# Down's first products by a second level of 2x2 blocks, shorter norm roots, and a shared last addition

## The chip, the cores and the metric

The kernel runs on one core of a Trainium2 chip. A core has five engines that run side by side: TensorE (PE in the profile, with its weight loads as PEld) for matmuls, VectorE (DVE) and ScalarE (ACT) for elementwise work, GpSimd (POOL), and SyncE (SP), which here only issues transfers. SP, ACT and POOL each have a queue of DMAs, served in order. Matmuls write to PSUM, everything else lives in SBUF or in DRAM. The metric is the device time of one execution in microseconds (us); lower is better. The three runs of the kernel before took 2181.01 to 2182.33 us, with a median of 2181.39.

## The reference

One residual block over 2048 tokens with 1024 channels, in float32:

```python
h = rmsnorm(x, norm_mix_pre)
u_pool, u_glu, g_a, g_b = split(h @ w_in)
branch_a = pool_mixer(u_pool, ...)        # windowed means, small maps, projection
branch_b = conformer_conv(u_glu, ...)     # GLU, causal convolution, layernorm, silu, projection
merged = sigmoid(g_a) * branch_a + sigmoid(g_b) * branch_b
x = x + rmsnorm(merged @ w_o, norm_mix_post)
h = rmsnorm(x, norm_mlp_pre)
f = square(relu(h @ w_up)) @ w_down       # 1024 -> 4096 -> 1024
x = x + rmsnorm(f, norm_mlp_post)
```
`rmsnorm(x, g)` is x divided by the root of (mean of squares + EPS), times g, with EPS = 1e-6.

## The kernel before

Data lie with channels on the 128 partitions and tokens along the row; a tile is 128x1024 float32, 512 KB. The tokens are two blocks b of 1024, each of two halves t of 512. A float32 product is made of three fast passes: each operand is split into a high part (a cast to fp32r on ACT, `wh` or a first `big`/`tr`) and a low part (the difference, a `sub` on DVE, `wl` or the second), and high x high, high x low, low x high are added in PSUM. `product` issues such a product of a 2x2 block of weights with a 1024-row slice of tokens: 24 matmuls of 128x512 (line 268).

Large matrix products are also made by a seven-product scheme over 2x2 blocks: seven products of sums and differences of blocks instead of eight products of blocks. `ORDER` gives the order of the seven. The products of w_in, of the output projection (wo) and of up are grouped so in `Octet`s, with block sums of the weights in `ws` tiles; up makes 8 octets for each b, and its relu-squared results go to DRAM as `fd[b, u, (m, t)]`, some of them already as the sums `t1`, `t2`, `t3`, `t4` that down wants.

Down runs for both blocks together. Its seven products i of the outer scheme are each summed over four slabs s of 1024 hidden rows, for two output halves o and two blocks b: 7 x 4 x 2 x 2 = 112 products. `SHARED` = (1, 5, 6, 3, 7) run for both b with one set of weights, `ALONE` = (4, 2) after them; the list `jobs` holds the order. `token_cells` loads and splits the token operands of a job two jobs ahead, `weight_down` the weights, `down_product` multiplies, and `last_product` joins the seven results into the four quarters c00, c01, c11, u. One job, `FILL`, is done early by `filler` to give PE work between wo and up of b=1; its result waits in DRAM. Half of the accumulators are pairs of `rb` tiles from the small PSUM pool, which is why products of down stand as `PE rb L268` in places.

The order of the work: the program is written in the main line of PE's products, and `ordered` and `mark` pin that line. Everything beside it (convolution, norms, `scales` for the mlp norm) is in `Lane`s of generators that `bg` moves on by some steps after every product. A scheduler orders each engine's instructions by priority; `tc.high_priority(offset=AHEAD)` moves a load or split ahead. Each engine and each queue then runs strictly in its order. `load` issues on SP's queue, `store` on ACT's, `aside` on POOL's. SBUF tiles come from pools with fixed numbers of buffers (`pbig` 28, `ptr` 9, `pfo` 5, `pwr` 4 for weights as loaded, `pwh` and `pwl` 3 for their parts).

Norm roots: `Squares` adds up squares, `root_acc` sums over partitions by 128x1 matmuls, `root_dve` makes 1/root by 8 to 14 small DVE operations (a bit trick and two refinements), `spread_dve` and `spread_pe` spread it over the partitions by matmuls with the identity, in a high and a low part. Finally `at_end` does the last product in two halves of 256 tokens with warming matmuls (`idle`) between, and then the last post norm and residual: for each of four output tiles a multiplication by the root (`times`) and an addition of x (`plus`), all on DVE, and a store on SP's queue.

## Time and profile before

| what | value |
|---|---|
| median of 3 runs | 2181.39 us (2181.01 to 2182.33) |
| the profiled execution's own time | 2180.6 us |
| its span in the trace | 2178.8 us |
| PE busy | 2159.4 us, 99% |
| DVE, ACT, POOL busy | 1614.7, 1017.8, 16.4 us |
| transferred | 552.33 MB, mean 253 GB/s |
| up of b=1 in the trace | 1243.27 to 1556.79 us |
| products i=1 of down | 1556.79 to 1632.95 us |

In rows of the profile, an operation reads `out<-in` by the program's names, with line, engine and shape; in square brackets stands the time that the engine was idle before it and what ended that. A row of a stretch gives its length, then busy time and instructions of PE, PEld, DVE, ACT and POOL, then the granted TensorE clock (1.00 is full), the busy share of the DMA engines and GB/s. The profiled execution took 2180.6 us, 1.8 more than the span of its instructions.

### The profile page before, as it was taken

Reading aid. Unit: us, or ns where it says so; the run is one execution under the profiler, and the core shown is the slowest. Engines: PE = TensorE matmul, PEld = TensorE weight load, DVE = VectorE, ACT = ScalarE, POOL = GpSimd, SP = SyncE. Lnnn points to the kernel's source line nnn. Section 1 sums busy time; section 2 is a strip of 40 time slices with the busy share of each in tenths; the row PEclk is TensorE's granted clock in tenths of the full one; section 3 lists DMA queues with packets and bytes.
Section 4 is the critical chain, followed back from the end, with each engine's and each line's share of the span. In section 5 each row is a group of like instructions: output and inputs, shape, how many; then the busy total and the mean of one; then the engine's idle time right before and its main releaser. Section 6 shows DMA issues by size and latency. Waiting matters only on the chain.

```text
span 2178.8 us, 25059 instructions
## 1 busy us (share of the span) xinstructions
PE 2159.4 (99%) x9678; PEld 1788.4 (82%) x9678; DVE 1614.7 (74%) x1593; ACT 1017.8 (47%) x1064; POOL 16.4 (1%) x39
## 2 busy tenths in 40 slices
PE   9999999999999999999999999999999999999998
PEld 7888888888888888888888878888888888888887
DVE  8997789998688998977757765756744746546786
ACT  6444454334543445555635775555622323334551
POOL 1000000000000000000000000000000000000000
PEclk9999999999999999999999999999999999999999
DMA  7688997778997788445787685644977875545882
GB/s 274 233 297 311 325 353 272 269 252 292 340 379 239 262 306 287 158 148 198 279 300 268 214 286 189 228 168 160 322 275 274 320 271 178 209 154 188 275 301 86
DMA packets 155625, 552.33 MB, mean 253 GB/s; under 512 B 17264, under 2 KB 19568, under 8 KB 155504
## 3 DMA queue, kind: packets, MB, share of 16 engines
q1 hardware_dynamic: 139696, 493.99, 63.7%
q10 hardware_dynamic: 12672, 46.14, 5.5%
q0 software_dynamic: 3136, 10.58, 1.3%
q8 instruction: 76, 1.25, 0.2%
q14 instruction: 45, 0.37, 0.1%
HBM read 366.00 MB, written 184.64 MB: 253 GB/s over the span
## 4 chain that ended last, share of the span: by engine, by line
PE 93%; DVE 3%; DMA 2%; issue 1%; ACT 1%; SPq 0%; DVEq 0%
PE up L268 26%; PE down L268 23%; PE wo L268 8%; PE ga L268 7%; PE gb L268 7%; PE glu L268 6%; PE rb L268 5%; PE B L268 4%; PE A L268 4%; PE pool L268 3%; DMA big<-xt 1%; PE rb L563 1%; DVE big L121 1%; PE mix L268 1%; DVE y L938 0%
## 5 line engine op out<-in xcount | busy, mean ns | idle before, releaser
L268 PE MATMUL up<-big,wh 128*128 128x512 f32 x1792 | 481.0, 390 | 2.2 <-DVE big L121 1.6
L268 PEld LDWEIGHTS up<-big,wh 128*128 128x128 f32 x1792 | 335.8, 188 | 74.0 <-DVE big L121 2.7
L225 ACT CAST wh<-wr 128x1024 fp32r<-128x1024 f32 x195 | 204.9, 1052 | 384.9 <-PE up L268 77.4
L938 DVE SCALAR_TENSOR_TENSOR y<-v,cst,y 128x1024 f32<-128x1024 f32 x240 | 307.2, 1280 | 2.8
L268 PE MATMUL up<-big,wl 128*128 128x512 f32 x896 | 276.1, 389 | 0.0
L268 PE MATMUL down<-big,wh 128*128 128x512 f32 x736 | 274.9, 389 | 0.0
L225 ACT CAST wh<-ws 128x1024 fp32r<-128x1024 f32 x126 | 132.4, 1052 | 252.8 <-PE up L268 63.6
L268 PE MATMUL down<-tr,wh 128*128 128x512 f32 x616 | 239.7, 389 | 0.0
L121 DVE TENSOR_TENSOR tr<-tr,big 128x1024 fp32r<-128x1024 f32 x100 | 120.5, 1222 | 117.3 <-ACT big L1730 116.8
L268 PE MATMUL down<-big,wl 128*128 128x512 f32 x664 | 204.5, 389 | 0.0
L121 DVE TENSOR_TENSOR wl<-ws,wh 128x1024 fp32r<-128x1024 f32 x118 | 143.9, 1220 | 75.5 <-ACT wh L225 75.3
L268 PEld LDWEIGHTS up<-big,wl 128*128 128x128 f32 x896 | 168.1, 188 | 34.8
L121 DVE TENSOR_TENSOR wl<-wr,wh 128x1024 fp32r<-128x1024 f32 x118 | 143.7, 1218 | 53.7 <-ACT wh L225 52.9
L1730 ACT CAST big<-tr 128x1024 fp32r<-128x1024 f32 x98 | 101.2, 1050 | 169.5 <-DMA tr<-fd 138.1
L268 PEld LDWEIGHTS down<-big,wh 128*128 128x128 f32 x736 | 138.2, 188 | 28.6
L268 PEld LDWEIGHTS down<-big,wl 128*128 128x128 f32 x664 | 124.6, 188 | 25.9
L268 PEld LDWEIGHTS down<-tr,wh 128*128 128x128 f32 x616 | 115.6, 188 | 24.0
L268 PE MATMUL wo<-big,wh 128*128 128x512 f32 x480 | 128.7, 390 | 0.0
L268 PE MATMUL glu<-big,wh 128*128 128x512 f32 x464 | 126.8, 394 | 1.2 <-DVE big L816 0.5
L268 PE MATMUL gb<-big,wh 128*128 128x512 f32 x448 | 120.0, 390 | 0.0
L268 PE MATMUL ga<-big,wh 128*128 128x512 f32 x448 | 120.0, 389 | 0.0
L268 PEld LDWEIGHTS wo<-big,wh 128*128 128x128 f32 x480 | 89.9, 188 | 18.5
(212 smaller groups left out, 3351.4 us busy)
## 6 DMA issues: line engine op xcount, KB each, us to landing
tr<-fd SPq DMA_DIRECT2D x110, 512.0 KB, 5.1
wr<-w_down SPq DMA_DIRECT2D x90, 512.0 KB, 5.8
wl<-kept SPq DMA_DIRECT2D x85, 512.0 KB, 4.6
kept<-wl SPq DMA_DIRECT2D x72, 512.0 KB, 6.1
wr<-w_up SPq DMA_DIRECT2D x64, 512.0 KB, 4.4
wr<-w_in SPq DMA_DIRECT2D x60, 512.0 KB, 5.3
fd<-tr ACTq DMA_DIRECT2D x54, 512.0 KB, 3.9
fd<-tr SPq DMA_DIRECT2D x46, 512.0 KB, 2.9
```

The lines of the kernel that those rows point to most:

```text
L121: return nc.vector.tensor_tensor(o, a, b, op=ALU.subtract)
L225: nc.scalar.copy(hi[:, :n], src[:, :n])
L268: i = nc.tensor.matmul(ps, w[wp][:, (at + k) * P : (at + k + 1) * P], rhs[k][xp], start=start and n == 0, stop=stop and n == len(order) - ...
L563: nc.tensor.matmul(st[:, at + g : at + g + 1], ss[:, g * P : (g + 1) * P], inv_n, start=start is None or (start and g == 0), stop=stop, sk ...
L938: nc.vector.scalar_tensor_tensor(acc, v[:, k : k + TB], wk, acc, op0=ALU.mult, op1=ALU.add)
L1730: nc.scalar.copy(hi, t)
```

## The change

Three parts. **Down.** The 16 products of i=1 (a matrix product of 4x2 slab parts by two token blocks) become a second level of the seven-product scheme: seven products `level_product`, each over two halves n, 14 in all, accumulated in three PSUM tiles x, y, z. Their weight sums are made by `level_weights`, a new generator ahead of `scales` in the lane beside up of b=1, and stored on POOL's queue; their token sums by `fetch_other` and `sink` during the octets of up of b=1 (T1 in octets 0 to 3; T2, T3, T4 in 4 to 7). `SHARED` loses 1, and the early job `FILL` is now (0, 7, 0), whose weights are differences; its result is added to `u` before the job (1, 3, 0). The `t4` sums are stored on POOL's queue instead of SP's, `pfo` has 6 buffers. **Roots.** EPS is added with the squares (or by `root_floor`, small matmuls into the same PSUM tile), `root_dve` takes its input from PSUM and has 8 operations, and one float32 matmul replaces the two fp32r ones in spreading. **The end.** Of the last half's four additions two go to GpSimd, one is split in two with a store for each half on ACT's and SP's queue, and two products by the root go to PSUM; four warming matmuls fewer.

```diff
-IDLE = (7, 9)
+IDLE = (7, 5)
...
+        h = step(ALU.mult, h, -0.5 * 0.375**3 * scale, a, "s2")
+        return step(ALU.add, h, 1.5 * 0.375 * scale, y, "sy")
+
+    def root_floor(st, b, t, at=0, n=G):
+
+        nc.tensor.matmul(
+            st[:, :n], f32(ident), q2[b, t][:, at : at + n], start=True, stop=False,
+            skip_group_check=True,
+        )
...
             for g in range(dg[0].shape[1]):
-                for i in (0, 1):
-                    j = nc.tensor.matmul(
-                        rb[:, g * P : (g + 1) * P], dg[i][:, g : g + 1].to_broadcast([P, P]), ident,
-                        start=g == 0 and i == 0, stop=i == 1, skip_group_check=True,
-                    )
...
+                j = nc.tensor.matmul(
+                    rb[:, g * P : (g + 1) * P], dg[0][:, g : g + 1].to_broadcast([P, P]),
+                    f32(ident), start=g == 0, stop=True, skip_group_check=True,
+                )
...
+            def fetch_other():
+                h = u - SLABS
+                for k, at in (
+                    (("T3", (1, h, (0, 0))), ("T2", (1, h, "T1")), ("T4", (0, u, (0, 0))))
+                    if u >= SLABS else (("T1", (0, u, (0, 0))),)
+                ):
+                    other[k] = fo()
+                    load(other[k], fd[at])
...
+                if b and (m, t) == (0, 0):
+                    for k, d in other.items():
+                        if k == "T4":
+                            sub(d, d, other["T2"])
+                        else:
+                            sub(d, o, d)
+                        keep(k, d, aside)
...
-    SHARED, ALONE = (1, 5, 6, 3, 7), (4, 2)
+    SHARED, ALONE = (5, 6, 3, 7), (4, 2)
...
-            for n in f.order:
+            for n in f.order[:2]:
                 times(1, n)
-                plus(1, n)
+                x = at(f.x[n], 1)
+                nc.gpsimd.tensor_tensor(x, x, at(f.ready[n], 1), op=ALU.add)
+                load(two(out[f.b, n, f.t])[:, :, HT:], x)
+            scaled = {}
+            for k, n in enumerate(f.order[2:]):
+                scaled[n] = ps[:, k * T : (k + 1) * T].rearrange("p (c t) -> p c t", c=2)
+                mul(
+                    scaled[n], at(f.ready[n], 1),
+                    rbs[1][:, :HT].unsqueeze(1).to_broadcast([P, 2, HT]),
+                )
...
+            for i, queue in enumerate((store, load)):
+                x = at(f.x[c], 1)[:, i]
+                add(x, x, scaled[c][:, i])
+                queue(two(out[f.b, c, f.t])[:, i, HT:], x)
...
-    FILL = jobs.pop(0)
...
+    FILL = (0, SHARED[-1], 0)
+    jobs.remove(FILL)
...
+    def level_product(p, w, cells):
+
+        a = {1: "x", 2: "z", 6: "x", 7: "x", 4: "x", 5: "y", 3: "y"}[p]
+        if p in (1, 2, 5):
+            sums_of[a] = psum("down")
+        ps = sums_of[a]
+        for n in (0, 1):
+            product(
+                ps, w[n], cells[2 * n : 2 * n + 2],
+                start=p in (1, 2, 5) and n == 0, stop=p in (2, 4, 3) and n == 1,
+            )
+            if n == 0:
+                bg()
...
-    then(lambda: lanes.extend([Lane(1, scales())]), octs[1])
+    then(lambda: lanes.extend([Lane(1, chain_of(level_weights(), scales()))]), octs[1], 1)
...
+    w = [level_weight(LEVEL[0], k) for k in (0, 1)]
+    here, coming = coming[0], coming[1:]
+    for n, p in enumerate(LEVEL):
+        with behind():
+            if n + 1 < len(LEVEL):
+                following = [level_weight(LEVEL[n + 1], k) for k in (0, 1)]
+                there = level_parts(coming.pop(0))
...
+            if n + 2 < len(LEVEL):
+                coming.append(level_loads(LEVEL[n + 2], (BIG, TR, BIG, TR, BIG)[n]))
...
+        level_product(p, w, here)
+        w, here = following, there
```

The change moves instructions on the engines. On DVE at the start of up of b=1, where PE waits for the operand differences (rows of L121 that write `big`), the order before has (L121 is a subtraction, L118 an addition, L124 a multiplication; a `tr` row makes a difference of token blocks, the `big` row behind it that operand's low part):

```order
L118 TENSOR_TENSOR big_9476<-big_9476,big_9463 128x1024
L121 TENSOR_TENSOR tr_9811<-big_9509,big_9003 128x1024
L121 TENSOR_TENSOR tr_9822<-big_9565,big_9085 128x1024
L121 TENSOR_TENSOR big_9814<-tr_9811,big_9813 128x1024
L121 TENSOR_TENSOR big_9825<-tr_9822,big_9824 128x1024
L118 TENSOR_TENSOR tr_9855<-tr_9798,tr_9853 128x1024
L121 TENSOR_TENSOR tr_9872<-big_9419,tr_9811 128x1024
L121 TENSOR_TENSOR tr_9883<-big_9463,tr_9822 128x1024
L121 TENSOR_TENSOR big_9875<-tr_9872,big_9874 128x1024
```
and in the changed kernel, at the same place:

```order
L118 TENSOR_TENSOR big_9422<-big_9422,big_9409 128x1024
L121 TENSOR_TENSOR fo_9674<-tr_9707,fo_9674 128x1024
L121 TENSOR_TENSOR tr_9762<-big_9455,big_8959 128x1024
L121 TENSOR_TENSOR tr_9773<-big_9511,big_9041 128x1024
L121 TENSOR_TENSOR big_9765<-tr_9762,big_9764 128x1024
L121 TENSOR_TENSOR big_9776<-tr_9773,big_9775 128x1024
L118 TENSOR_TENSOR tr_9806<-tr_9747,tr_9804 128x1024
L121 TENSOR_TENSOR tr_9826<-big_9369,tr_9762 128x1024
L121 TENSOR_TENSOR tr_9837<-big_9409,tr_9773 128x1024
L121 TENSOR_TENSOR fo_9749<-tr_9806,fo_9749 128x1024
L121 TENSOR_TENSOR big_9829<-tr_9826,big_9828 128x1024
```
The two `fo` rows, the T1 sums of octets 0 and 1, stand between the operands that PE waits for.

On DVE in the first stage of down, the order of one level and the start of the next in the changed kernel (`tr` and `big` rows are the low parts of a level's four token operands, `wl` those of its two weights):

```order
L121 TENSOR_TENSOR tr_12108<-tr_12108,big_12178 128x1024
L121 TENSOR_TENSOR tr_12109<-tr_12109,big_12181 128x1024
L121 TENSOR_TENSOR tr_12110<-tr_12110,big_12184 128x1024
L121 TENSOR_TENSOR wl_12169<-wr_12166,wh_12168 128x1024
L121 TENSOR_TENSOR tr_12111<-tr_12111,big_12187 128x1024
L121 TENSOR_TENSOR wl_12175<-wr_12172,wh_12174 128x1024
L121 TENSOR_TENSOR big_12190<-big_12190,big_12260 128x1024
L121 TENSOR_TENSOR big_12191<-big_12191,big_12263 128x1024
```
Six splits come for each two products there; before, a job of two products had two token splits, and two weight splits for each two jobs.

On DVE at the end, before, from the end of the last root (`sy`, `sp`, `sq`) to the second of four tiles:

```order
L124 TENSOR_TENSOR sy_16352<-sy_16350,q_11137 128x2
L634 CAST sp_16354<-sy_16352 128x2
L121 TENSOR_TENSOR sq_16355<-sy_16352,sp_16354 128x2
L124 TENSOR_TENSOR big_13626<-big_13626,rb_16358 128x2x256
L118 TENSOR_TENSOR big_15547<-big_15547,big_13626 128x2x256
L124 TENSOR_TENSOR big_13654<-big_13654,rb_16358 128x2x256
L118 TENSOR_TENSOR big_15549<-big_15549,big_13654 128x2x256
```
and in the changed kernel (the two additions that are missing, to `big_15599` and `big_15601`, are the last rows on POOL):

```order
L601 SCALAR_TENSOR_TENSOR s_3286_16371<-s_3285_16369,rb_16334 128x2
L601 SCALAR_TENSOR_TENSOR sy_16373<-s_3286_16371,sy_16367 128x2
L124 TENSOR_TENSOR big_13744<-big_13744,rb_16375 128x2x256
L124 TENSOR_TENSOR big_13772<-big_13772,rb_16375 128x2x256
L124 TENSOR_TENSOR down_16094<-big_12246,rb_16375 128x512
L124 TENSOR_TENSOR down_16094<-big_12329,rb_16375 128x512
L118 TENSOR_TENSOR big_15603<-big_15603,down_16094 128x2x256
L118 TENSOR_TENSOR big_15605<-big_15605,down_16094 128x256 x2
```
The four multiplications now stand together, and two additions follow them on DVE.

More of the change, by code (lines that the diff above doesn't have):

```diff
@@ L1762, in to @@
                 mark(add(c[:, h], of[:, h], p))
[L1764 to L1771 removed]
+        if i == 5:
             taken(c11)
@@ new lines, in level_weight, with level_loads @@
+    def level_weight(p, n):
+        with tc.high_priority(offset=AHEAD):
+            t = mk(p_wr, "wr")
+            o = {1: 2 * n, 2: 2 * (n + 2), 4: 2 * (n + 2) + 1}.get(p)
+            load(t, level[p, n] if o is None else w_down[o, 0])
+            return split_w(t)
+    def level_loads(p, home):
+        b, at, k = {
+            1: (0, 0, (0, 0)), 2: (0, SLABS, (0, 0)), 3: (1, SLABS, (0, 0)),
+            5: (1, 0, "T1"), 6: (1, SLABS, "T2"), 7: (1, SLABS, "T3"), 4: (1, SLABS, "T4"),
+        }[p]
+        with tc.high_priority(offset=AHEAD):
+            los = [mk(*home, F32R) for _ in range(SLABS)]
+            for u, lo in enumerate(los):
+                load(f32(lo), fd[b, u + at, k])
+        return los
```

184 lines of the change are left out of this document (116 added, 68 removed).

## The prediction

> **What bounds the kernel now.** I read the page's busy shares and its chain first, then the chain over the place of the change, then PE's waits, and last the engines' load stage by stage.
>
> ```profile
> span 2178.8 us, 25059 instructions
> PE 2159.4 (99%) x9678; PEld 1788.4 (82%) x9678; DVE 1614.7 (74%) x1593; ACT 1017.8 (47%) x1064; POOL 16.4 (1%) x39
> PE 93%; DVE 3%; DMA 2%; issue 1%; ACT 1%; SPq 0%; DVEq 0%
> ```
> PE is busy for all but 19 us of the span and carries 93% of the chain that ended last: the kernel is a queue of matmuls, and a matmul taken out of it is worth its own length as long as its neighbours' operands are there in time. The chain through the first stage of down (columns: start, length, what) prices it:
>
> ```profile
> 1556.79 5.44 PE down L268 x24
> 1562.23 5.44 PE rb L268 x24
> 1567.67 16.32 PE down L268 x72
> ...
> 1627.51 5.44 PE rb L268 x24
> ```
> A product is 24 matmuls in 5.44 us, 0.2267 us each, with no gap to the next one. Products i=1 run here from 1556.79 to 1632.95: fourteen of them in 76.16 us (the other two are the filler's). PE's waits (total, times, longest) show where it does starve:
>
> ```profile
> PE rb L563 <- DVE tr L118: 1.9, 1, 1.9
> PE rb L654 <- DVE sp L634: 1.6, 2, 1.0
> PE up L268 <- DVE big L121: 1.6, 2, 0.8
> ```
> All of it is small. The load by stretch (sum; PE, PEld, DVE, ACT, POOL busy; granted clock, DMA share, GB/s) tells what room is left; the rows are the start of up of b=1, the rest of that up, stage i=1 of down, the rest of down but for its end, and the 22 us in which the DMA moved most:
>
> ```profile
> 1243.27:1297.67 54.40, 52.63 (x236) 42.51 (x235) 43.76 (x48) 42.76 (x49) 0.00 (x0) 1.00 0.83 290
> 1297.67:1556.79 259.12, 259.12 (x1160) 214.86 (x1159) 161.18 (x156) 148.37 (x148) 0.00 (x0) 1.00 0.58 208
> 1556.79:1632.95 76.16, 76.16 (x337) 63.06 (x337) 37.17 (x32) 19.96 (x22) 0.00 (x0) 1.00 0.79 288
> 1632.95:1981.11 348.16, 348.16 (x1537) 288.29 (x1537) 188.98 (x161) 114.66 (x117) 0.00 (x0) 1.00 0.65 227
> 620.76:642.52 21.76, 21.76 (x97) 18.02 (x96) 19.30 (x17) 7.04 (x7) 0.00 (x0) 1.00 1.02 403
> ```
> In the stages that the change loads, DVE was 49% (37.17 of 76.16) and 62% (161.18 of 259.12) busy. Only the start of up is near its limit, 43.76 of 54.40 us, and there PE did wait.
>
> **Products of down.** Sixteen products i=1 become fourteen: two fewer are 48 matmuls, 48 x 0.2267 = **-10.9 us**, and no product has to be added for it. The filler keeps a product for each o, now i=7.
>
> What must hide is the feeding of the seven new levels. In 76 us the queues now move 28 token tiles, 14 weight tiles and about five for the next stage, 47 of 512 KB, 24.6 MB or 324 GB/s; the stage moved 288 and the fullest row above 403, so I cost the transfers at nothing. DVE's work there, by the prices
>
> ```profile
> L121 DVE TENSOR_TENSOR wl<-wr,wh 128x1024 fp32r<-128x1024 f32 x118 | 143.7, 1218 | 53.7 <-ACT wh L225 52.9 <-DMA kept<-wl 0.6
> L225 ACT CAST wh<-wr 128x1024 fp32r<-128x1024 f32 x195 | 204.9, 1052 | 384.9 <-PE up L268 77.4
> ```
> is 42 splits, 3 additions and about 6 operations for the next stage, 51 x 1.22 = 62 us (82%); ACT has 42 casts, 4 copies and 6 more, 52 x 1.05 = 55 us (72%). Both fit, but each level needs four token and two weight splits within two products (10.88 us; DVE 7.3 us), the loads come one or two levels ahead, and every queue works in order: a load that is late delays the splits behind it, and those delay PE. The stretch above with DVE at 80% cost PE 1.77 us (54.40 - 52.63); so between 0 and 2 us for levels and seams, I take **+1.0**.
>
> The sums made in up of b=1 are 16 token subtractions, 16 loads and 16 stores; the weight sums are 8 operations, 8 loads and 8 stores (the stores on POOL's queue, 0.54 us to issue by the row
>
> ```profile
> L131 POOL DMA_DIRECT2D x1d<-big x8 | 4.3, 535 | 134.6 <-DVE big L118 108.3 <-DVE s L124 14.4 <-DVE sq L121 12.0
> ```
> and it has nothing else there). That is 24 x 1.22 = 29 us of DVE, of which 2 lie in the crowded start; the rest lifts 161 to about 188 of 259 us, 73%, and the DMA by 48 x 0.524 MB / 259 us = 97 to 305 GB/s. Hidden, by the same bounds. At the crowded start it is different:
>
> ```profile
> 1252.73 0.50 PE L268 MATMUL up<-big,wh 128*128 128x512 f32 x1 [0.80 <-DVE big L121]
> 1275.15 1.64 PE L268 MATMUL up<-big,wh 128*128 128x512 f32 x5 [0.75 <-DVE big L121]
> ```
> DVE's order now has the T1 subtraction of the first two octets among the operand differences that these matmuls wait for, and two more subtractions for the filler's weights shortly before: 4 x 1.22 = 4.9 us more; 6 small operations fewer (the roots, below) give back 1.2. Of the 3.7 us between, PE pays what its lead doesn't cover: 0 to 3.7, I take **+1.5**, since PE waited twice in 54 us and so had a lead elsewhere.
>
> The remaining edits (squares in place, `t4` stored by POOL's queue instead of SP's, a sixth `pfo` buffer, the loads of the first jobs put behind the main work) cost nothing under PE's run of products without a gap in that row of 348.16 us; without that cover each is one operation of 0.5 to 1.2 us.
>
> **Shorter roots.** A root is a chain of operations 0.2 us apart while PE goes on with other matmuls, except in two places. In the opening PE waits for the first one:
>
> ```profile
> 28.02 0.17 DVE L634 CAST sp<-sy 128x4 fp32r<-128x4 f32 x1
> 28.34 0.30 PE L654 MATMUL rb<-ident,sp 128*128 128x128 f32 x1 [1.04 <-DVE sp L634]
> ```
> Three operations fewer (the addition of EPS, cast and difference) are 0.6 us; DVE bounds the next 25 us too, and two roots lie there, so 0.6 to 1.5: **-0.8**. The tail's root is counted with the tail.
>
> Spreading takes 28 fp32 matmuls of 128x128 instead of 56 fp32r ones. At the start of up PE has both of the nearest kinds, each between its own start and the next row's:
>
> ```profile
> 1244.63 1.02 PE L563 MATMUL rb<-inv_d,tr 128*128 128x1 f32 x8
> 1245.51 0.96 PE L268 MATMUL up<-big,wl 128*128 128x512 f32 x3
> ...
> 1249.28 0.22 PE L654 MATMUL rb<-ident,sp 128*128 128x128 f32 x1
> ...
> 1250.12 0.45 PE L268 MATMUL up<-big,wh 128*128 128x512 f32 x1
> ```
> Eight of the old kind take 0.84 us, 0.105 each; eight fp32 ones of a single column take 0.88, 0.11 each. The new kind has fp32 data and 128 columns: at least 0.11, and bounded above by four of the old, 0.42. So 28 x (0.11 to 0.42) - 56 x 0.105: -3 to +6 us. I take **0**, two of the old for one new, which lies nearer to the rows than to the multiple. By the Trainium skill ("FP8 and Floating Point Precision") true fp32 is four passes; four passes over 128 columns at the long matmul's rate (0.2267 / 4 = 0.057) would be 0.23 and the sum +0.2. No row here shows it.
>
> The floor that replaces EPS in the mlp roots is five fp32 matmuls of 2 or 4 columns, 0.11 to 0.42 each by the same bounds: 0.5 to 2.1, **+0.9**.
>
> **The tail.** DVE's end and the last store:
>
> ```profile
> 2166.38 0.16 DVE L124 TENSOR_TENSOR s<-rb,q 128x2 f32<-128x2 f32 x1 [1.56 <-PE rb L1891]
> ...
> 2168.95 0.16 DVE L121 TENSOR_TENSOR sq<-sy,sp 128x2 fp32r<-128x2 f32 x1
> 2169.75 0.69 DVE L124 TENSOR_TENSOR big<-big,rb 128x512 f32<-128x512 f32 x1 [0.64 <-PE rb L654]
> ...
> 2174.44 0.69 DVE L118 TENSOR_TENSOR big<-big,big 128x512 f32<-128x512 f32 x1
> ```
> The root's 14 operations run 2166.38 to 2169.11, 0.195 us apart; they become 8: -1.17. The eight operations behind it, 5.38 us, become four multiplications, one addition and two halves, 4 x 0.66 + 0.66 + 2 x 0.4 = 4.1: -1.3, if GpSimd's two additions end by then. The first can start 0.7 us into it, so two of up to 1.7 us fit. The nearest rows:
>
> ```profile
> L724 POOL CAST ident<-tr 128x128 fp32r<-128x128 f32 x1 | 0.3, 302 | 0.0
> L186 POOL MEMSET inv_d<- 128x1 f32 x1 | 0.1, 99 | 0.0
> ```
> A cast of 128 costs 0.20 over the fixed 0.1, so 512 elements cost 0.9 us, and 1.7 if a second input doubles it: it just fits. With the root the tail gives -1.17 - 1.3, less 0.2 for two floors in PE's way: **-2.3**. The Trainium skill ("GPSIMD Engine Reference", 3.1 Elementwise) has the addition at 2.6 cycles of 1.2 GHz an element, estimated 1.1 us here, inside these bounds. The same page (8. Key points) says that GpSimd and DVE contend for SBUF when DVE reads two SBUF inputs; the DVE operations beside it here have one input in PSUM, so by that rule nothing is lost, and if it held anyway rival C below is the outcome. Four warming matmuls fewer cost nothing: DVE's root covers them.
>
> **The sum.** -10.9 + 1.0 + 1.5 - 0.8 + 0 + 0.9 - 2.3 = -10.6. The profiled execution took 2180.6 us, so 2170.0; it lies 0.8 below the median of the runs, 2181.39, so **2170.8** there. With no cost and the larger gains (-1.5 opening, -2.5 tail) it is 2166.5; a third of the spread's -3 gives 2165.5. What a measurement can tell from no change is about 0.2%, 4.4 us.
>
> **Rivals.**
> A, the other side: the levels are fed too slowly. Their loads stand on one queue with the stores of up's last octets, and if they get only the mean of the span,
>
> ```profile
> HBM read 366.00 MB, written 184.64 MB: 253 GB/s over the span
> ```
> 24.6 MB take 97 us, not 76, and PE waits for 21: 2192. It ends slower once the stage costs 15 us or more, that is below 270 GB/s. Against it: this stage had 288 and DMA idle at its end, and 403 was sustained for 22 us.
>
> B: stalls of PE that also cost clock. One is in the trace (the last two rows: stretch as above):
>
> ```profile
> 762.02 1.02 PE L563 MATMUL rb<-inv_d,tr 128*128 128x1 f32 x8 [1.87 <-DVE tr L118]
> 758.00:763.00 5.00, 3.13 (x19) 2.47 (x18) 3.83 (x4) 0.00 (x0) 0.00 (x0) 1.00 1.02 412
> 763.00:768.00 5.00, 5.00 (x16) 3.98 (x16) 2.94 (x7) 0.47 (x1) 0.53 (x1) 0.66 0.53 216
> ```
> 1.87 us of waiting, then five at a granted clock of 0.66: 16 matmuls where 22 fit, so 3.7 us in all. Two such, at the start of up and at a seam of the levels, make 2171 - 1 + 7.4 = 2177. The Trainium skill ("TensorE: Matmul & The Clock Gate", What's actually happening) wants about 3.4 us of idleness before the clock falls; by that none of PE's waits would cost it, but the trace shows a fall after less, and the measurement decides.
>
> C: GpSimd's additions take over 1.9 us beside DVE, and the tail ends no sooner than before but for the root: 2172.
>
> D: the change doesn't do what it says. The program has 48 fewer product matmuls, so it could be so only if PE waited for them elsewhere, which is A.
>
> **How the numbers follow.** My forecast (2167 to 2174) 0.60, C 0.12 (2172 to 2175), B 0.13 (2175 to 2179), A 0.15, half of which ends above 2185.8 and half between 2177 and it. Faster by over 0.2% means below 2177.0: 0.60 + 0.12 + half of B 0.07 = 0.79; slower 0.08; within 0.13. The range is 2165.5 (the costs nothing, as above) to 2181.5, which takes in B with some of the spread's +6 and a quarter of A, and leaves out about 0.1.
>
> **What would show it.** 48 fewer matmuls and one 5.44 us product after another through the seven levels (right), or PE waits there for DVE's splits or for loads at level seams (A, B), with granted clock under 1 behind them. PE's waits for operands at the start of up above 1.6 us (the +1.5). GpSimd's additions under 1.7 us each and DVE's last operation some 4.1 us after the spread (C otherwise). Spread matmuls of about 0.23 us. Wrong above all if the start of up, whose DVE order changes, falls behind for longer than one octet.

## The result, and the profile after

The changed kernel takes 2171.94 us, the median of ten runs (2167.19 to 2180.25); the kernel before, in ten runs beside it, 2181.55. The ratio is 0.9962 with a 95% interval from 0.9952 to 0.9973, so the change saves 5.9 to 10.5 us, 8.3 in the middle (9.6 by the medians). The forecast was 2170.8, 10.6 below the kernel before.

The profiled execution of the changed kernel has a span of 2168.5 us against 2178.8. Its page, with span and busy times, and the chain of work through the end of up and the first stage of down:

```profile
span 2168.5 us, 25149 instructions
PE 2147.6 (99%) x9636; PEld 1779.4 (82%) x9636; DVE 1654.6 (76%) x1577; ACT 1037.7 (48%) x1083; POOL 34.9 (2%) x71
```
```profile
1529.95 27.65 PE up L268 x122
1557.61 92.48 PE down L268 x408
1650.09 5.44 PE rb L268 x24
```
PE is still the bound, with 11.8 us less work. The 408 matmuls from 1557.61 on are seventeen products of 5.44 us without any gap: fourteen of the seven levels and three of the next stage. The feed of the levels is hidden completely. The stretches (the start of up of b=1, the rest of it, the level stage) show by how much:

```profile
1241.50:1300.00 58.50, 55.03 (x248) 44.52 (x247) 49.70 (x51) 44.39 (x50) 3.20 (x6) 1.00 0.96 347
1300.00:1557.61 257.61, 256.60 (x1148) 212.94 (x1147) 172.51 (x153) 139.83 (x139) 9.59 (x18) 1.00 0.72 271
1557.61:1633.77 76.16, 76.16 (x337) 63.08 (x337) 56.83 (x50) 44.27 (x45) 0.00 (x0) 1.00 0.84 332
```
In the level stage DVE is busy 56.83 of 76.16 us and the DMA moves 332 GB/s with a share of 0.84, where 62 us and 324 GB/s had been estimated. The start of up is where PE starves: it lacks 3.47 of 58.50 us there (1.77 of 54.40 before). PE's waits in the whole of up of b=1 say what for:

```profile
PE up L268 <- DVE big L121: 2.7, 2, 1.7
...
PE up L268 <- DVE tr L118: 1.0, 1, 1.0
...
PE up L268 <- ACT big L218: 0.8, 1, 0.8
```

Cut at three places that every trace has (the first product of up of b=1, the first product of down, and the addition with which DVE takes over the last product), the span of each kernel falls into four parts. Rows for `roots_tail`, `level_only`, `up_order` and `best` belong to the experiments below; all are single profiled executions, in us. (Starts are those of PE's rows, 0.16 us ahead of the chain's.)

| kernel | until up of b=1 | up of b=1 | down | the end | span |
|---|---|---|---|---|---|
| before | 1243.27 | 313.36 | 606.90 | 15.27 | 2178.8 |
| after | 1241.34 | 316.11 | 597.30 | 13.75 | 2168.5 |
| roots_tail | 1239.38 | 314.81 | 607.85 | 13.76 | 2175.8 |
| level_only | 1241.35 | 314.44 | 596.02 | 15.39 | 2167.2 |
| up_order | 1238.72 | 314.02 | 596.97 | 13.79 | 2163.5 |
| best | 1243.00 | 313.03 | 596.97 | 13.80 | 2166.8 |

Before to after: -1.93, +2.75, -9.60 and -1.52, in sum -10.3. A single pair of traces says little about the first column: among the kernels with the roots of the changed one, whose work is nearly the same there, it runs from 1237.03 (`tail_queue`) to 1244.57 (`one_ahead`). The last two columns repeat: down is 596.96 to 596.98 in six traces with the code of the changed kernel there, 597.30 in its own and 597.77 in `tail_queue`. Up repeats only where the clock holds. With the same code there it took 315.94 to 316.11 us in three traces (the changed kernel's, `slow_root`'s and `tail_dve`'s), but 319.85 in `tail_queue`, where the granted clock fell twice behind PE's waits. One of the two stretches:

```profile
1270.00:1275.00 5.00, 4.45 (x12) 3.31 (x13) 5.00 (x6) 4.68 (x5) 0.29 (x1) 0.67 0.95 309
```
A granted clock of 0.67 (third figure from the end) over 5 us is a loss of about 1.7 us; the other fall is near 1475 us.

### The profile page after: what moved, and what is told of

The parts are those of the page before. It is cut to its first block, busy times and chain, and to the rows that moved or that the text cites. A ratio compares the mean times of both kernels' runs of the same rounds, so it can differ in the third digit from the quotient of the medians.

```text
span 2168.5 us, 25149 instructions
## 1 busy us (share of the span) xinstructions
PE 2147.6 (99%) x9636; PEld 1779.4 (82%) x9636; DVE 1654.6 (76%) x1577; ACT 1037.7 (48%) x1083; POOL 34.9 (2%) x71
## 4 chain that ended last, share of the span: by engine, by line
PE 82%; issue 10%; DVE 3%; DMA 3%; ACT 1%; POOL 0%; SPq 0%; DVEq 0%; POOLq 0%
PE down L268 24%; PE up L268 17%; PE wo L268 8%; PE gb L268 7%; PE ga L268 7%; PE glu L268 6%; PE B L268 4%; PE rb L268 4%; PE A L268 4%; PE pool L268 1%; DVE y L935 1%; DMA wl<-kept 1%; DVE tr L118 1%; PE rb L563 1%; PE mix L268 1%
## 5 line engine op out<-in xcount | busy, mean ns | idle before, releaser
L268 PE MATMUL down<-big,wh 128*128 128x512 f32 x856 | 296.7, 390 | 0.0
L268 PE MATMUL down<-big,wl 128*128 128x512 f32 x704 | 216.8, 389 | 0.0
L268 PE MATMUL down<-tr,wh 128*128 128x512 f32 x552 | 214.9, 389 | 0.0
L121 DVE TENSOR_TENSOR wl<-ws,wh 128x1024 fp32r<-128x1024 f32 x120 | 146.5, 1222 | 66.7 <-ACT wh L225 66.6
L268 PEld LDWEIGHTS down<-big,wh 128*128 128x128 f32 x856 | 160.7, 188 | 33.7 <-DVE big L121 0.4
L121 DVE TENSOR_TENSOR wl<-wr,wh 128x1024 fp32r<-128x1024 f32 x122 | 148.7, 1220 | 43.3 <-ACT wh L225 42.6
L121 DVE TENSOR_TENSOR tr<-tr,big 128x1024 fp32r<-128x1024 f32 x92 | 110.4, 1222 | 75.2 <-ACT big L1748 69.5
L268 PEld LDWEIGHTS down<-big,wl 128*128 128x128 f32 x704 | 132.2, 188 | 27.5
L1748 ACT CAST big<-tr 128x1024 fp32r<-128x1024 f32 x82 | 84.5, 1050 | 113.1 <-DMA tr<-fd 97.7
L121 DVE TENSOR_TENSOR big<-big,big 128x1024 fp32r<-128x1024 f32 (+1 forms) x90 | 108.0, 1221 | 33.8 <-ACT big L1074 14.5
L268 PEld LDWEIGHTS down<-tr,wh 128*128 128x128 f32 x552 | 103.7, 188 | 21.4
```

The lines of the kernel that those rows point to most:

```text
L121: return nc.vector.tensor_tensor(o, a, b, op=ALU.subtract)
L268: i = nc.tensor.matmul(ps, w[wp][:, (at + k) * P : (at + k + 1) * P], rhs[k][xp], start=start and n == 0, stop=stop and n == len(order) - ...
L1748: nc.scalar.copy(hi, t)
```

## The experiments

### One half of the change at a time

`roots_tail` is the kernel before with the roots and the end of the changed one, `level_only` the kernel before with down, its sums and the filler of the changed one. The diffs here give parts of the edits.

```diff
 # roots_tail, against the kernel after
-    SHARED, ALONE = (5, 6, 3, 7), (4, 2)
+    SHARED, ALONE = (1, 5, 6, 3, 7), (4, 2)
...
-    FILL = (0, SHARED[-1], 0)
-    jobs.remove(FILL)
+    FILL = jobs.pop(0)
```

> The kernel before with the shorter roots and the shared last addition alone; down and up as before. Theory (the parts add up, and the opening's gain belongs to the root): the stage that follows the opening starts 2.9 us sooner than before, with no stretch of granted clock below 1 between 25 and 40 us; floors and spreads give about 2 us back until the end, the tail gains 1.5: in all 1.5 to 2.5 us less than before. The first wait at the start of up of b=1 is 1.7 us as in the changed kernel, if the multiplication that now stands ahead of it on VectorE comes from the shorter root, and 0.8 if it comes from the sums. Rival (the opening's gain is chance, or comes from down's part through the order of the instructions): the opening is as before, and the whole kernel is 0.5 us faster to 1 us slower.

Ratio to before 0.9991 (0.9983 to 1.0000), so 0 to 3.7 us are saved. The first pool product starts at 91.53, 2.15 us sooner than before (93.68) and not 2.9, without a fall of the clock. The three waits at the start of up, and further down those of `level_only`, with the sixth octet's:

```profile
1249.74 0.50 PE L268 MATMUL up<-big,wh 128*128 128x512 f32 x1 [1.73 <-DVE big L121]
1271.47 0.50 PE L268 MATMUL up<-big,wh 128*128 128x512 f32 x1 [0.77 <-ACT big L218]
1272.73 1.64 PE L268 MATMUL up<-big,wh 128*128 128x512 f32 x5 [0.76 <-DVE big L121]
```

```diff
 # level_only, against the kernel after
-        f = p_const.tile([P, 2 * G], F32, tag=f"q{b}", name=f"q{b}")
-        nc.vector.tensor_scalar(f, st[:, : 2 * G], EPS**0.5 * SQ, None, op0=ALU.mult)
-        mul(f, f, f)
+        r = root_dve(st[:, : 2 * G])
+        q = p_const.tile([P, 2 * G], F32, tag=f"q{b}", name=f"q{b}")
+        mul(q, r, r)
```

> The kernel before with the second level in down and its sums alone; roots and the end as before. Theory (the parts add up): 10.9 us less in down and no wait in its fourteen level products (408 matmuls and more from its start without a gap); the start of up of b=1 loses 0.8 us in its second pair of waits and 1.0 near the sixth octet: in all 8.5 to 9.5 us less than before. Rival (the two parts need each other, since the roots' saved operations made room for the sums): waits in up of b=1 above 3 us in all, and less than 8 us gained.

Ratio 0.9953 (0.9939 to 0.9967).

```profile
1250.78 0.50 PE L268 MATMUL up<-big,wh 128*128 128x512 f32 x1 [0.81 <-DVE big L121]
1271.92 0.49 PE L268 MATMUL up<-big,wh 128*128 128x512 f32 x1 [0.21 <-ACT big L218]
1273.38 1.63 PE L268 MATMUL up<-big,wh 128*128 128x512 f32 x5 [0.97 <-DVE big L121]
1473.09 1.65 PE L268 MATMUL up<-big,wh 128*128 128x512 f32 x6 [0.88 <-DVE tr L118]
```

By the table the halves add up: in up +1.45 and +1.08 for +2.75 together, in down +0.95 and -10.88 for -9.60, at the end -1.51 and +0.12 for -1.52. `level_only` gains its two products to the hundredth. The surprise is in the waits: the two that grew at the start of up come almost wholly with the shorter *roots* (1.73 and 0.77, as in the changed kernel), not with the sums, which had been blamed for them; the sums bring 0.2 in the third row and the new wait near 1473. Behind the opening the roots and the end together cost 0.9 us (1.45 + 0.95 - 1.51). By the times, too, the second level alone does no worse than the whole change (0.9953 against 0.9962, with overlapping intervals): that the roots and the end add to the gain is not shown.

### Sums moved out of the crowded start

```diff
+                if u < 2:
+                    return
...
+    def level_first():
+        for u in (0, 1):
+            d, e = fo(), fo()
+            load(d, fd[1, u, (0, 0)])
+            load(e, fd[0, u, (0, 0)])
+            yield 2
+            sub(e, d, e)
...
-    then(lambda: lanes.extend([Lane(1, chain_of(level_weights(), scales()))]), octs[1], 1)
+    then(lambda: lanes.extend([Lane(1, chain_of(level_weights(), level_first(), scales()))]), octs[1], 1)
```

> The changed kernel with the T1 sums of the first two octets of up of b=1 taken out of their place between the operands and made in the lane behind the weight sums, from DRAM (two more loads). Theory (these two subtractions cause the added part of the second pair of waits): 0.77 and 0.96 us fall back to about 0.2 and 0.75, 0.8 us less, and the first wait of 1.73 stays. Rival (order and transfers at the start of up cause them): the pair stays within 0.2 us of 1.73 in sum.

The waits are 1.73, 0.77 and 0.76: only 0.2 went, and the pair now reads as in `roots_tail`. The rival was right; but for these 0.2 us, T1 is not what PE waits for. The time (2170.68, ratio 0.9956, 0.9942 to 0.9971) can't be told from the changed kernel's; nor does it price T1 alone, since a wait of 1.12 us for the sums of a root came up at 1558.88 and the one near the sixth octet went. What PE does wait for is an order. On DVE before (the first two rows) and after (the next two, with the row of PE that waits), behind the root that both have just spread:

```profile
1250.32 1.22 DVE L124 TENSOR_TENSOR big<-big,rb 128x1024 f32<-128x1024 f32 x1 [0.34 <-PE rb L654]
1251.46 1.22 DVE L121 TENSOR_TENSOR big<-big,big 128x1024 fp32r<-128x1024 f32 x1
```
```profile
1248.18 2.35 DVE L124 TENSOR_TENSOR big<-big,rb 128x1024 f32<-128x1024 f32 x2 [0.73 <-PE rb L645]
1250.44 1.22 DVE L121 TENSOR_TENSOR big<-big,big 128x1024 fp32r<-128x1024 f32 x1
1251.72 0.51 PE L268 MATMUL up<-big,wh 128*128 128x512 f32 x1 [1.73 <-DVE big L121]
```
The low part for which PE waits (L121) stands behind two multiplications instead of one, and those wait for the spread (0.73 us). Its own high part had been cast by ACT in time (1247.30 to 1248.34). That this order comes with the roots is shown by `roots_tail`; which of their edits brings it, the fewer operations or the new spreading, was not taken apart.

### That order, kept

```diff
-            mul(two(o[c, t]), two(o[c, t]), per_token(rbs[t]))
+            i = mul(two(o[c, t]), two(o[c, t]), per_token(rbs[t]))
+            if t:
+                if not behind_of:
+                    behind_of.append(low[0])
+                tc.add_manual_dep(i.ins, behind_of[0].name, NOSYNC, reason="in order")
...
```
`low[0]` is the low part that was split last.

> The changed kernel with one order kept on VectorE: the multiplications of the second half's tiles by the root come behind the low part of the second octet product's operand. Theory (PE's first wait at the start of up of b=1 is 1.73 us because the shorter root let two multiplications be put ahead of that low part, whose high part was not ready in the scheduler's order): this wait falls from 1.73 to under 0.2 us, and the pair at the second octet does not grow by more than 0.5. Rival (VectorE is simply full there, and the wait moves): the three waits keep a sum of 3.0 to 3.5 us.

```profile
1268.66 0.50 PE L270 MATMUL up<-big,wh 128*128 128x512 f32 x1 [0.27 <-ACT big L218]
1270.31 1.63 PE L270 MATMUL up<-big,wh 128*128 128x512 f32 x5 [1.14 <-DVE big L121]
1469.65 1.66 PE L270 MATMUL up<-big,wh 128*128 128x512 f32 x6 [0.52 <-DVE tr L118]
```
The first wait is gone, and the pair is 1.41 instead of 1.73: the three fell from 3.46 to 1.41 us (one run, 2165.27 us). DVE had the time; it was spent in the wrong order.

### Both places in up

The wait near the sixth octet is a chain of queues in the changed kernel's trace (SP first, then DVE):

```profile
1455.34 0.39 SPq L127 DMA_DIRECT2D fo<-fd  x1
1467.17 0.33 SPq L127 DMA_DIRECT2D wr<-w_up  x1
```
```profile
1464.78 1.23 DVE L121 TENSOR_TENSOR fo<-fo,fo 128x1024 f32<-128x1024 f32 x1 [3.64 <-DMA fd<-fo]
1465.92 1.22 DVE L121 TENSOR_TENSOR wl<-wr,wh 128x1024 fp32r<-128x1024 f32 x1
1472.35 1.22 DVE L118 TENSOR_TENSOR ws<-wr,wr 128x1024 f32<-128x1024 f32 x1 [5.21 <-DMA wr<-w_up]
1473.49 1.22 DVE L118 TENSOR_TENSOR tr<-up,tr 128x1024 f32<-128x1024 f32 x1
```
DVE stands still for 3.64 us ahead of the T4 subtraction. The row names a store, but the subtraction's own input was issued at 1455.34 and took 9.3 us to land, until about 1464.6, and the subtraction begins at 1464.78: it waited for that load. Behind it stands the split of a weight, which frees the buffer of the next weight at 1467.14; SP's load of that weight goes out at 1467.17, its sum is made at 1472.35, and the addition that frees PE's accumulator comes last. The wait that PE has from it differs between executions of the same code, from 0.54 to 1.59 us, and is missing in `double_loads` (and in `t1_late`). `best` has the order above and puts the T4 subtraction behind the next addition of its octet:

```diff
-                        if k == "T4":
-                            sub(d, d, other["T2"])
...
+                if "T4" in other and len(f) == 2:
+                    i = sub(other["T4"], other["T4"], other["T2"])
+                    tc.add_manual_dep(
+                        i.ins, marks[mybir.EngineType.DVE].name, NOSYNC, reason="in order"
+                    )
+                    keep("T4", other["T4"], aside)
```

> The changed kernel with the order of up_order and with the T4 sums put behind the next addition of their octet on VectorE, so that the load that they wait for no longer holds up the weights behind them. Theory (the waits in up of b=1 come from these two places): the first wait of 1.73 and the one of 1.01 near the sixth octet go, 2.7 us and now and then a halved clock of 1.7: a median 2.5 to 4 us below the changed kernel's. Rival (the waits are handed on within up): not more than 1 us below it.

Both waits are gone, and up of b=1 takes 313.03 us, less than before the change (313.04 in `best_warm` below, which has both edits too). The median is 2167.97 us, ratio 0.9939 (0.9925 to 0.9952): 10 to 16 us below the kernel before, and by the medians 4.0 us below the changed kernel, though the two intervals touch.

### The opening and the clock

Three multiplications by 1 behind the first root make it as long as before.

```diff
-            self.dg = spread_dve(root_dve(self.st[:, :G]), None)
+            y = root_dve(self.st[:, :G])
+            if self.t == 0:
+                for k in range(3):
+                    y2 = small(("s1", "s2")[k % 2], G)
+                    nc.vector.tensor_scalar(y2, y, 1.0, None, op0=ALU.mult)
+                    y = y2
+            self.dg = spread_dve(y, None)
```

> The changed kernel with three small VectorE operations put behind the first root of the opening, so that it is as long as before. Theory (the root's chain is worth its operations, 0.2 us each, and the rest of the opening's gain was a halved clock that befell the profiled execution of before): PE's wait for the root grows from 0.48 to about 1.07 us, and the first pool product starts 0.6 us later than in the changed kernel, counted from the end of the first waits; 1.7 more only if a stretch of granted clock below 1 shows between 25 and 40 us. Rival (the length of the root itself decides whether the clock falls): such a stretch shows, and the pool product starts 2 to 3 us later.

PE's wait for the root and the stretch behind it, in `slow_root` (one run, 2168.61 us), then those of the changed kernel and of `level_only` (which has the long root of before):

```profile
28.63 1.13 PE L645 MATMUL rb<-ident,s 128*128 128x128 f32 x8 [1.36 <-DVE s L790]
30.00:35.00 5.00, 5.00 (x18) 4.10 (x19) 5.00 (x7) 2.48 (x3) 0.53 (x1) 0.66 0.82 275
```
```profile
27.87 1.13 PE L645 MATMUL rb<-ident,sy 128*128 128x128 f32 x8 [0.48 <-DVE sy L601]
30.00:35.00 5.00, 5.00 (x23) 4.10 (x22) 5.00 (x8) 2.10 (x2) 0.00 (x0) 1.00 0.86 305
```
```profile
29.07 0.30 PE L654 MATMUL rb<-ident,sp 128*128 128x128 f32 x1 [0.91 <-DVE sp L634]
30.00:35.00 5.00, 5.00 (x28) 4.31 (x28) 5.00 (x7) 2.54 (x3) 0.53 (x1) 1.00 0.62 229
```
The granted clock fell in `slow_root`, as it had in the profiled execution of before (0.67 in its row from 30 to 35 us), and the pool product came 2.05 us later than in the changed kernel (92.82 against 90.77), about 2.2 when the first waits are taken off. PE's wait grew by 0.88, more than the 0.6 expected. Both forecasts allow for that outcome, the first by its 1.7. In `level_only`, with a wait of 0.91, the clock did not fall. So a stretch at reduced clock may come on top of the wait, or not. A row of 5 us at 0.66 is 3.4 us at half clock, a loss of 1.7 us. In the nine traces in which this wait is 0.46 to 0.80 us it never came; of the three with 0.91 to 1.36 us it came in two (the thirteenth, `tail_dve`, has no such wait; its clock had fallen near 12 us, behind waits of 1.64 and 0.49). That the longer wait brings the fall is suggested by these counts, not shown. The opening's gain in the traces, -2.91 us to the first pool product, is then about 1.2 from the root and the waits around it and 1.7 from a clock that fell in one of the two executions. `level_only`, which has the long root and no fall, agrees: counted from the last of PE's first waits (11.37, and 10.68 in the changed kernel) its pool product (92.86) comes 1.4 us later than the changed kernel's.

### Filling a wait

The same question at the place near 760 us, where PE waits 1.87 us before the change and 1.81 after: eight matmuls of ones ahead of the root's own.

```diff
+                    if ts == (1,):
+                        idle(WARM, root_psum(), sq[1].last)
                     st = root_pe(*ss, inv_n=inv_d)
...
```

> The kernel best with eight matmuls of ones put into PE's queue shortly ahead of the matmuls of the mixer norm's second root of block 0, at the place near 760 us where PE waits some 1.9 us for VectorE; their results are not used. Theory (a wait of PE there costs its own length and, in most executions, a stretch of 3.4 us at half clock behind it, 1.7 us more): the 1.8 us of matmuls fill the wait, so they cost nothing themselves, the wait falls below 0.4 us, no row of 5 us behind it shows a granted clock below 1, and the median is 1 to 1.7 us below that of best. Rival (the halved clock is chance, and has nothing to do with the wait): the clock falls there as often, and the time is that of best or up to 1.8 us above it.

```profile
755.20 2.01 PE L577 MATMUL rb<-ones 128*128 128x512 f32 x8
...
759.34 1.02 PE L566 MATMUL rb<-inv_d,tr 128*128 128x1 f32 x8 [1.43 <-DVE tr L696]
762.00:767.00 5.00, 5.00 (x19) 4.00 (x18) 3.57 (x7) 1.63 (x3) 0.53 (x1) 0.77 0.58 238
```
The eight matmuls run just ahead of the wait (three of the next product stand between), but the wait was still 1.43 us, against 1.88 in `best`: VectorE's chain there starts when a load lands (757.37, and 759.49 in `best`), and without the eight PE would have reached the place that much sooner ahead of it. The clock fell as it did in `best`. The median, 2167.46 us (ratio 0.9941, 0.9927 to 0.9954), is that of `best`. It shows neither that the wait lowers the clock nor that it doesn't; the wait wasn't filled. A trace without the fall at this place is that of `level_only`, with a wait of 1.95 us:

```profile
761.63 1.02 PE L563 MATMUL rb<-inv_d,tr 128*128 128x1 f32 x8 [1.95 <-DVE tr L118]
762.00:767.00 5.00, 5.00 (x26) 4.23 (x27) 4.54 (x9) 1.45 (x2) 0.53 (x1) 1.00 0.60 194
```
Ten of the thirteen traces have a fall there, after waits of 1.14 to 2.19 us; three, with 1.5, 1.7 and 1.95, have none. The Trainium skill ("TensorE: Matmul & The Clock Gate", What's actually happening) describes a window of about 3.4 us that runs free of the program. The falls here are 3.4 us long, which agrees; that a wait well short of such a window is enough, the traces alone show, and why it is so in some executions only stays open.

### The end

`tail_dve` puts the last half's eight operations back on DVE in pairs, with the new root.

```diff
-            for n in f.order[:2]:
+            for n in f.order:
                 times(1, n)
-                x = at(f.x[n], 1)
-                nc.gpsimd.tensor_tensor(x, x, at(f.ready[n], 1), op=ALU.add)
...
+                plus(1, n)
```

> The changed kernel with the last half's four multiplications and four additions on VectorE in pairs, each with its store on SP's queue, as before the change. Theory (the sharing shortens VectorE's end by 1.3 us, of which the bunched transfers take back 0.55): from the first of these multiplications to the end of the span 9.05 us instead of 8.31. Rival (all of the tail's gain is the root's): 8.3.

From the first multiplication at 2160.55 to the end of its span at 2169.7 it takes 9.15 us (one run, 2171.47 us), against 8.31 in the changed kernel (2160.19 to 2168.5). So the sharing is worth 0.84, and the root the rest of 1.52. The changed kernel's rows on DVE, POOL and SP:

```profile
2160.19 1.28 DVE L124 TENSOR_TENSOR big<-big,rb 128x512 f32<-128x512 f32 x2 [0.87 <-PE rb L645]
2161.39 1.49 DVE L124 TENSOR_TENSOR down<-big,rb 128x512 f32<-128x512 f32 x2
2162.92 1.35 DVE L118 TENSOR_TENSOR big<-big,down 128x512 f32<-128x512 f32 x3
```
```profile
2161.02 2.49 POOL L1961 TENSOR_TENSOR big<-big,big 128x512 f32<-128x512 f32 x2 [426.76 <-DVE big L124]
2150.44 14.95 SPq L127 DMA_DIRECT2D out<-big  x8
```
DVE's part is 4.08 us (2160.19 to 2164.27), GpSimd's additions take 1.25 us each, and both fit. But SP issues its last stores until 2165.39, 1.12 us behind DVE; before, 0.56 (2175.69 and 2175.13). `tail_queue` sends GpSimd's two tiles by ACT's queue:

```diff
                 nc.gpsimd.tensor_tensor(x, x, at(f.ready[n], 1), op=ALU.add)
-                load(two(out[f.b, n, f.t])[:, :, HT:], x)
+                store(two(out[f.b, n, f.t])[:, :, HT:], x)
```

> The changed kernel with the stores of GpSimd's two outputs on ACT's queue instead of SP's. Theory (SP's queue bounds the end: its last three issues follow GpSimd's second addition one after another, and the last ends 1.1 us after VectorE's last operation): from VectorE's last addition of the last product's first half to the end of the span 13.0 us instead of 13.75, with the last issue under 0.6 us behind VectorE's last operation. Rival (the transfers themselves bound the end): 13.75 as now, whatever queue issues them.

```profile
2150.34 14.62 SPq L127 DMA_DIRECT2D out<-big  x6
```
SP's last issue now ends 0.79 us behind DVE's end at 2164.17, but the span ends no sooner: 13.85 us from DVE's last product addition (2154.65 to 2168.5), against 13.75. The expected 0.6 was not reached either, but the rival was right: the stores now take longer to land, 3.0 us for the last half tile instead of 2.5. What the DMA moved from 2160 to 2169 us, in 40 slices, in the changed kernel and in `tail_queue`:

```profile
GB/s 0 0 0 0 0 0 0 0 0 0 0 0 0 0 0 109 391 373 287 5 0 332 387 382 369 392 387 382 369 391 105 0 0 0 0 0 0 0 0 0
```
```profile
GB/s 0 0 0 0 0 0 0 0 0 0 0 0 0 0 0 82 378 396 301 9 36 341 387 387 373 382 396 382 369 378 64 0 0 0 0 0 0 0 0 0
```
In both the transfers run at one rate without a pause from about 2164.7 to 2166.9, and 1.6 us later the span ends: the tiles are finished within some 2 us of each other, and moving them sets the end. The time was 2170.29 us (ratio 0.9958, 0.9944 to 0.9972).

### How much room the level stage has

In `one_ahead` the token operands of a level are loaded one level ahead, not two.

```diff
-                there = level_parts(coming.pop(0))
+                there = level_parts(
+                    coming.pop(0) if n == 0 else level_loads(LEVEL[n + 1], (BIG, TR, BIG, TR, BIG)[n - 1])
+                )
...
```

> The changed kernel with the token operands of the level products loaded one level ahead instead of two. Theory (the level stage has no wait because its loads come two levels, some 20 us, ahead of their use, where they have slack; what counts is that they land and are split within the 10.88 us of one level): four loads and four splits now have to follow each other within one level, and PE waits 1 to 4 us at most of the seams, 5 to 20 us in all. Rival (the feed has room enough in any order): under 1 us of waits in the stage.

The fourteen products again ran without a gap; the rival was right for the levels. Only behind them, where the next stage's loads come late, PE waited:

```profile
1665.94 0.50 PE L268 MATMUL down<-big,wh 128*128 128x512 f32 x1 [2.37 <-ACT big L1748]
1667.27 0.50 PE L268 MATMUL down<-big,wh 128*128 128x512 f32 x1 [0.82 <-DVE big L121]
```
Its one run took 2182.52 us, beside 2179.24 of one run of the kernel before; 3.2 us of that are these waits, with a fall of the clock behind them, and its first part and up were long too (1244.57 and 319.57 us, two falls in that up).

`double_loads` loads every token operand of the levels twice.

```diff
                 load(f32(lo), fd[b, u + at, k])
+                load(f32(lo), fd[b, u + at, k])
```

> The changed kernel with every token operand of the levels loaded twice into the same tile (28 loads more). Theory (the prediction's rival A is a matter of the rate: 47 tiles in 76 us are 324 GB/s, and 75 tiles would be 517 GB/s, above the 420 or so that the DMA shows in its fullest stretches): PE waits in the level stage, which takes 15 to 30 us longer, at 380 to 420 GB/s. Rival (the stage has much more room, since the queues fill up ahead of it): under 5 us longer.

Its one run took 2206.21 us, beside 2179.24. PE's waits between 1540 and 1700 us, and the stretch of the level stage:

```profile
PE down L268 <- ACT wh L225: 11.5, 4, 4.1
PE up L268 <- ACT tr L439: 5.0, 1, 5.0
```
```profile
1557.00:1633.00 76.00, 65.35 (x269) 52.51 (x269) 44.40 (x38) 38.78 (x38) 0.00 (x0) 0.93 0.93 344
```
The fourteen products took some 96 us instead of 76.2, as expected: about 12.6 us of waits, and the granted clock below 1 behind them. But the test mixes two causes. The rate is 344 GB/s at a DMA share of 0.93, below the 380 to 420 expected, and the second load of a tile waits for the first: between 1540 and 1660 us SP's queue stood for 70.9 us on loads of these tiles, against 11.7 in the changed kernel. So rival A's mechanism exists (late loads that hold up the ones behind them on a queue), and here PE meets it at the weights' splits (11.5 us of waits at the casts `wh`); at which rate alone it would begin stays open.

## Why the prediction was right or wrong

**The two products (-10.9): right.** `level_only` gains 10.88 us in down.

**Levels and seams (+1.0): too much.** No wait in the levels; 0.33 us among the products behind them (16.65 us instead of 16.32 for three at 1655.53), which six other traces of that code don't have. DVE's estimate of 62 us was 56.83, ACT's of 55 us 44.27. Rival A did not come true, and with room to spare: even with loads one level ahead the levels ran without a gap.

**The start of up (+1.5): the size right, the cause wrong.** The three waits grew from 1.77 to 3.46 us, by 1.7. The step that failed was to add the four new subtractions' time and take off the shorter root's; `roots_tail` has 1.5 of the 1.7 without any sum, and `t1_late` gives back only 0.2. The roots' edits, counted there as a gain of 1.2 us, changed the order in which DVE's work was laid out, and that cost more than they gave. That 1.5 had been forecast for the sum is luck.

**What lay in the cover of the rest of up (0): missed.** DVE had room on the mean (172.51 of 257.61 us, where 188 had been estimated), but one subtraction that waited 3.64 us for its data stood in an ordered queue ahead of a weight's split, for 1.0 us of PE. The mean load of a stretch doesn't show it; `best` takes it away.

**The opening (-0.8): under.** The trace has -2.91 to the first pool product. The root's own part is 1.2 to 1.4; the rest was clock, which the price by DVE's operations left out, although rival B had priced just that at another place. The rows from there to up of b=1 give 0.98 us back, spread over small waits that differ from execution to execution, so the part's true value isn't known to better than some 2 us, if that.

**Spreading (0): right but at the end.** The four fp32 matmuls of one spread (two rows each in the trace) take 0.91 us, 0.23 each, where eight fp32r took 0.84. That agrees with the four passes of the Trainium skill ("FP8 and Floating Point Precision", TensorE Precision Notes), which over 128 columns had been estimated at 0.23. With 0.2267, 28 spreading matmuls for 56 old ones of 0.105 cost 0.5 us in sum (28 x 0.2267 - 56 x 0.105), not the +0.2 given ahead. Where DVE has nothing but the spread to wait for, at the end, it waits 0.87 us for it instead of 0.64.

```profile
1247.25 0.91 PE rb L645 x8
1998.57 0.12 PE rb L618 x2
1998.69 0.89 PE rb L563 x8
```

**The floors (+0.9): right in sum.** Down has +0.95 in `roots_tail`: a floor costs 0.12 (second row), less than the 0.18 that was taken, and the sums behind it 0.89 instead of 0.79.

**The end (-2.3): too much by 0.8.** DVE's operations gave what was said (14 to 8 in the root, 4.08 us for 4.1), GpSimd's addition at 1.25 us lies between the bounds of 0.9 and 1.7, a little above the 1.1 estimated from the Trainium skill ("GPSIMD Engine Reference", 3.1 Elementwise). What failed is the step from DVE's end to the end of the span, 0.56 of the 0.8: the stores were left as they were, and now come in a bunch. The other 0.23 is the spread, which had been put at nothing.

That the traces' -10.3 lies so near the forecast -10.6 is in part luck. The execution profiled before had a fall of the clock at the opening, and the one after had not; without its 1.7 us the traces give -8.6, near the 8.3 of the runs. Against that the forecast saved 2 us too much: 1.25 in up and 0.8 at the end, and 0.6 up to up of b=1, where the waits between took back what the root gave; down was 0.6 better than its terms. In the main the forecast case came true. B came true in part. Waits at the start of up grew by 1.7 us, and a fall of the clock followed the second pair in three of the eight traces in which the first wait is 1.73 (`t1_late`, `tail_queue`, `one_ahead`). This may be where the spread of 13 us between the ten runs comes from: the traces of single executions, `double_loads` apart, have none to four falls.

## What to carry to other kernels

When PE is full, count what leaves its queue, and then ask of each new instruction not how long it is but what stands behind it in its engine's order. A shorter chain beside the critical path can cost more than it gives if the order in which a scheduler lays out the work changes with it; so compare the order at the places where PE already waits. When several engines share the last work, price the moving of the results too, since they then arrive together. And when traces of single executions are compared, note first which falls of the clock only one of them has.

## What was unexpected of the hardware

Some waits of PE that are well under 3.4 us are followed by 3.4 us at half clock: 0.66 or 0.67 in a row of 5 us, 1.7 us lost. Length alone does not decide it. Near 760 us, where eight matmuls of one column (1.02 us) follow the wait, it came after waits of 1.14 to 2.19 us in ten traces of thirteen. The wait of 1.73 us at the start of up, with full matmuls behind it, has none in any of the eight traces that have it. Two waits of 0.77 and 0.76 to 0.97 us close to each other, some 22 us later, were followed by one in three of these eight. Whether small matmuls count as idleness here was not tested.

Fourteen products with 42 operand splits and a DMA share of 0.84 run beside PE without a single gap. The start of up, with a share of 0.96, had waits, but most of them went with an order on DVE, not with fewer transfers.
